# A streaming maximum over rows: one store moved to the end, the last row cut into two chained halves, all loads at one row pitch

## Chip, cores and metric

The kernel runs on one core of one Trainium2 chip. The metric is device time in microseconds (us); a profile of one execution goes with each kernel.

## The reference

```python
def setup_inputs():
    batch, seq, dim = 32, 512, 1024
    return {"x": np.random.randn(batch, seq, dim).astype(np.float32)}

def reference(x):
    return np.max(x, axis=-1).astype(np.float32)
```

This is 16384 rows of 1024 floats (4 KB each): 67.11 MB are read, 64 KB are written.

## The kernel before

Each of the 128 partitions takes 128 rows, in two blocks: 112 neighbouring rows (so neighbouring partitions lie 112 x 4 KB = 448 KB apart in `x`; this distance is called the pitch), then 16 rows (pitch 64 KB). A block is loaded in pieces of falling size through a ring of 46 rows per partition. VectorE reduces each piece. Each block has one store.

```python
BLOCKS = [
    [14, 14, 12, 11, 9, 8, 8, 7, 6, 5, 4, 4, 4, 3, 3],
    [2, 2, 2, 2, 2, 1, 1, 1, 1, 1, 1],
]
RING = 46
# ... (pools, shapes)
    at = first = 0
    for loads in BLOCKS:
        S = sum(loads)
        xb = xf[first * P:(first + S) * P, :].rearrange("(p i) d -> p i d", p=P)
        b = 0
        for g in loads:
            if at + g > RING:
                at = 0
            xc = ring[:, at:at + g, :]
            nc.sync.dma_start(out=xc, in_=xb[:, b:b + g, :])
            nc.vector.reduce_max(out=res[:, first + b:first + b + g], in_=xc, axis=X)
            at += g
            b += g
        dst = bass.AP(tensor=of.tensor, offset=of.offset + first * P, ap=[[S, P], [1, S]])
        nc.scalar.dma_start(out=dst, in_=res[:, first:first + S])
        first += S
```

## Time and profile before

| | before |
|---|---|
| time, median | 165.1 us (165.01 to 165.19, 6 runs) |
| span of the profiled run | 163.3 us |
| first load lands | 20.1 us after the start of the span |
| last store issued, landed | 160.91, 162.33 us |

In the profile lines of this document DVE is VectorE, SPq the queue that issues the loads, ACTq the one that issues the stores, and L50 a line of the kernel's source; `...` stands between lines of different views or for lines left out.

How to read the table: almost the whole span is one stream of loads that keeps all 16 DMA engines busy. Three stages can be told apart: how late the first load lands, how long the stream takes from its first landing to its last, and the tail after the last landing (last reduction, last store).

### The profile page before, as it was taken

What the parts mean: (1) busy time and instruction counts of PE and PEld (TensorE: products, weight loads), DVE (VectorE), ACT (ScalarE), POOL (GpSimd) and SP (SyncE); (2) the same over time, 40 slices, a digit from 0 to 9 for tenths busy, and PEclk for the clock granted to TensorE, in tenths of its full rate; (3) what the DMA queues carried; (4) which work ended last, traced back from release to release, by engine and by line L of the source; (5) the groups of instructions that cost most, each with busy time, mean ns of one, the idle gap of its engine ahead of it and who ended that gap; (6) DMA issues with size and microseconds to landing.
All of it is one profiled execution on the core that took longest, in us unless ns stands there. A gap on an engine that the chain in (4) does not pass through costs nothing.

```text
span 163.3 us, 109 instructions
## 1 busy us (share of the span) xinstructions
DVE 138.5 (85%) x26; POOL 0.2 (0%) x4
## 2 busy tenths in 40 slices
DVE  0000099969999999999999999999999999999994
POOL 0000000000000000000000000000000000000000
DMA  6999999998899897999989999999999999999980
GB/s 225 449 449 449 449 449 449 449 417 385 385 409 522 353 530 321 433 433 441 473 385 473 425 449 400 434 395 451 413 425 433 429 414 418 425 421 419 404 357 2
DMA packets 4032, 67.18 MB, mean 411 GB/s; under 512 B 704, under 2 KB 704, under 8 KB 1472
## 3 DMA queue, kind: packets, MB, share of 16 engines
q1 hardware_dynamic: 3744, 67.11, 96.4%
q10 hardware_dynamic: 288, 0.07, 0.2%
HBM read 67.11 MB, written 0.07 MB: 411 GB/s over the span
## 4 chain that ended last, share of the span: by engine, by line
DMA 57%; DVE 40%; DVEq 1%; SPq 0%; issue 0%
DMA ring<-in_x_dram 57%; DVE res L50 40%; DVEq L82 1%; SPq L49 0%
## 5 line engine op out<-in xcount | busy, mean ns | idle before, releaser
L50 DVE TENSOR_REDUCE res<-ring 128x1 f32<-128x1024 f32 (+11 forms) x26 | 138.5, 5396 | 22.4 <-DMA ring<-in_x_dram 22.4
L71 POOL MEMSET const-bfloat16-1.0<- 128x1 bf16 x1 | 0.1, 101 | 0.0
L71 POOL MEMSET const-uint8-127<- 128x1 uint8 x1 | 0.1, 101 | 0.0
L71 POOL MEMSET const-float32-0.0<- 128x1 f32 x1 | 0.1, 98 | 0.2 <-issue 0.2
L71 POOL MEMSET const-float32-1.0<- 128x1 f32 x1 | 0.1, 98 | 0.0
## 6 DMA issues: line engine op xcount, KB each, us to landing
ring<-in_x_dram SPq DMA_DIRECT2D x2, 7168.0 KB, 27.6
ring<-in_x_dram SPq DMA_DIRECT2D x2, 4096.0 KB, 31.6
ring<-in_x_dram SPq DMA_DIRECT2D x1, 6144.0 KB, 49.9
ring<-in_x_dram SPq DMA_DIRECT2D x3, 2048.0 KB, 36.8
ring<-in_x_dram SPq DMA_DIRECT2D x1, 5632.0 KB, 29.7
ring<-in_x_dram SPq DMA_DIRECT2D x5, 1024.0 KB, 24.6
ring<-in_x_dram SPq DMA_DIRECT2D x1, 4608.0 KB, 23.7
ring<-in_x_dram SPq DMA_DIRECT2D x1, 3584.0 KB, 38.4
```

Source lines behind the costliest of these rows:

```text
L50: nc.vector.reduce_max(out=res[:, first + b:first + b + g], in_=xc, axis=X)
L71: nc = _bacc.Bacc("TRN2", target_bir_lowering=False, num_devices=1)
L82: with _tile.TileContext(nc) as tc:
```

## The change

It has four parts. All loads get one pitch of 512 KB (128 rows per partition in one run). The last two-row and single-row loads are cut finer, so that eight single rows precede the last one. The last row of each partition is loaded as two halves into different buffers; the first half's maximum is written just ahead of the second half, so that the second reduction (513 elements) takes it in. And the first store now holds 127 of the 128 results per partition, so that it can't go out before the loads are nearly over; the last store then writes one float per partition. The intent is a stream without a store in it and less work after the last landing.

```diff
-BLOCKS = [
-    [14, 14, 12, 11, 9, 8, 8, 7, 6, 5, 4, 4, 4, 3, 3],
-    [2, 2, 2, 2, 2, 1, 1, 1, 1, 1, 1],
-]
-RING = 46
+ROWS = [14, 13, 11, 11, 9, 8, 8, 7, 6, 5, 5, 4, 4, 3, 3, 2, 2, 2, 2, 1, 1, 1, 1, 1, 1, 1, 1]
+RING = 45
+RUN = 128
 ...
+    xr = xf[:RUN * P, :].rearrange("(p i) d -> p i d", p=P)
+    out_r = bass.AP(tensor=of.tensor, offset=of.offset, ap=[[RUN, P], [1, RUN]])
+    if RUN == I:
+        x_last, out_last = xr[:, I - 1, :], out_r[:, I - 1:]
+    else:
+        x_last = xf[RUN * P:, :]
+        out_last = bass.AP(tensor=of.tensor, offset=of.offset + RUN * P, ap=[[1, P], [1, 1]])
 ...
+    PAD = 16
+    tail = once.tile([P, PAD + H], F32)
 ...   (loop over ROWS: load and reduce as before)
+    half = ring[:, at, :H]
+    nc.sync.dma_start(out=half, in_=x_last[:, :H])
+    nc.sync.dma_start(out=tail[:, PAD:], in_=x_last[:, H:])
+    nc.scalar.dma_start(out=out_r[:, :I - 1], in_=res[:, :I - 1])
+    nc.vector.reduce_max(out=tail[:, PAD - 1:PAD], in_=half, axis=X)
+    nc.vector.reduce_max(out=res[:, I - 1:], in_=tail[:, PAD - 1:], axis=X)
+    nc.scalar.dma_start(out=out_last, in_=res[:, I - 1:])
```

More of the change, by code (lines that the diff above doesn't have):

```diff
@@ L32 @@
     N, D = xf.shape
+    H = D // 2
     I = N // P
     of = out.flatten_outer_dims()
+    assert sum(ROWS) == I - 1 and RUN >= I - 1
+    xr = xf[:RUN * P, :].rearrange("(p i) d -> p i d", p=P)
[5 more added lines that the diff above has]
+        out_last = bass.AP(tensor=of.tensor, offset=of.offset + RUN * P, ap=[[1, P], [1, 1]])
     once = ctx.enter_context(tc.tile_pool(name="once", bufs=1))
@@ L38 @@
     res = once.tile([P, I], F32)
-    at = first = 0
-    for loads in BLOCKS:
-        S = sum(loads)
-        xb = xf[first * P:(first + S) * P, :].rearrange("(p i) d -> p i d", p=P)
-        b = 0
-        for g in loads:
-            if at + g > RING:
-                at = 0
-            xc = ring[:, at:at + g, :]
-            nc.sync.dma_start(out=xc, in_=xb[:, b:b + g, :])
-            nc.vector.reduce_max(out=res[:, first + b:first + b + g], in_=xc, axis=X)
-            at += g
-            b += g
-        dst = bass.AP(tensor=of.tensor, offset=of.offset + first * P, ap=[[S, P], [1, S]])
-        nc.scalar.dma_start(out=dst, in_=res[:, first:first + S])
-        first += S
-    assert first == I
+    PAD = 16
+    tail = once.tile([P, PAD + H], F32)
+    b = at = 0
+    for g in ROWS:
+        if at + g > RING:
+            at = 0
+        xc = ring[:, at:at + g, :]
+        nc.sync.dma_start(out=xc, in_=xr[:, b:b + g, :])
+        nc.vector.reduce_max(out=res[:, b:b + g], in_=xc, axis=X)
+        at += g
+        b += g
+    if at + 1 > RING:
+        at = 0
+    half = ring[:, at, :H]
[5 more added lines that the diff above has]
+    nc.scalar.dma_start(out=out_last, in_=res[:, I - 1:])
 _INS = ['x']
```

## The prediction

> **What bounds the kernel now.** I read the page first, then the chain in order of time, then windows over the loading stage, then the timeline and issues of the last microseconds. One core, no matmul: only VectorE (DVE), the load queue (issued from SP) and the store queue (issued from ACT) matter.
>
> The page of the kernel before, busy tenths and queues:
>
> ```profile
> span 163.3 us, 109 instructions
> DVE 138.5 (85%) x26; POOL 0.2 (0%) x4
> ...
> DMA  6999999998899897999989999999999999999980
> ...
> q1 hardware_dynamic: 3744, 67.11, 96.4%
> q10 hardware_dynamic: 288, 0.07, 0.2%
> ```
>
> The reader should see a DMA row without a hole from the first slice to the last but one, and the load queue q1 holding 96.4% of the time of all 16 engines. DVE works 138.5 of 163.3 us: it has slack overall. The chain of waits, in order of time, seems to say otherwise:
>
> ```profile
> 1.15 35.88 DMA ring<-in_x_dram
> ...
> 37.05 58.02 DVE res L50 x5
> ...
> 95.08 36.77 DMA ring<-in_x_dram
> ...
> 131.87 19.94 DMA ring<-in_x_dram
> ...
> 151.84 7.92 DVE res L50 x6
> 159.75 1.13 DVEq L82
> ```
>
> Its 58 us of DVE in the middle are not what sets the time: DVE lags behind the stream there, but the DMA engines never go idle, and at 95.08 the chain is back on the DMA. Only the end counts: from 151.84 on DVE reduces back to back until the last row. Windows (busy columns are DVE and POOL; the last three numbers are clock, share of the 16 DMA engines, GB/s):
>
> ```profile
> 40.00:95.00 55.00, 55.00 (x5) 0.00 (x0) 1.00 1.00 433
> 95.00:132.00 37.00, 36.78 (x8) 0.00 (x0) 1.00 0.99 425
> 132.00:139.00 7.00, 7.00 (x2) 0.00 (x0) 1.00 1.00 421
> 142.00:149.30 7.30, 7.30 (x4) 0.00 (x0) 1.00 1.02 422
> ...
> 152.00:158.00 6.00, 6.00 (x5) 0.00 (x0) 1.00 1.03 410
> ```
>
> The engines are always full; the rate sinks only because loads get smaller, from 433 GB/s for loads of 7 to 14 rows a partition to 410 for single rows. So the time is: about 158 us of saturated loading, then a tail of the last reduction and the last store. The tail, from the timeline and the issues of the last load pair and the last store:
>
> ```profile
> 151.84 9.04 DVE L50 TENSOR_REDUCE res<-ring 128x2 f32<-128x2048 f32 x7 [0.19 <-DMA ring<-in_x_dram]
> ...
> ring<-in_x_dram SPq DMA_DIRECT2D x2, 512.0 KB, 9.1
> ...
> 160.91 0.34 ACTq L54 DMA_DIRECT2D out_dram<-res x1
> ...
> out_dram<-res ACTq DMA_DIRECT2D x1, 8.0 KB, 1.4
> ```
>
> The last two loads were issued at 149.53 and 149.90 and took 9.1 us each in the median (8.7 for the first alone, so 9.5 for the second): the last lands at T = 159.4 to 159.5. The last reduction runs from 159.67 to 160.88, the store is issued at 160.91 and lands 1.4 us later, at 162.3; closing work fills the rest to 163.3.
>
> **What the Trainium skill says.** First, "DMA: Bandwidth & Descriptors", section "Where 436 GB/s comes from": 16 ports give 435.2 GB/s. The trace agrees, 433 GB/s with large loads, so the stream can't get much faster: 67.11 MB at 435.2 would take 154.2 us. Second, same page, section "Latency and other measured facts": copies from HBM to HBM at a row pitch of 512 KiB ran at 207 GB/s per direction, against 214 for a padded pitch (and 164 at 2 MiB); it calls the mechanism an inference. No run here shows a pitch of 512 KB; the trace shows pitches of 448 KB (112 rows of 4 KB, the first block) and 64 KB (the second block), both at full engine share. Third, same page, section "Anatomy of one DMA — SWDGE (gpsimd) path": a fixed cost of about 2 us, most of it the receipt of the write. The store here, from another queue, took 1.4 us. Fourth, "VectorE: DVE Perf Modes", section "The perf-mode tier table": a tensor reduction has only the 1x mode. The trace agrees:
>
> ```profile
> L50 DVE TENSOR_REDUCE res<-ring 128x14 f32<-128x14336 f32 x2 | 30.2, 15086 | 22.0 <-DMA ring<-in_x_dram 22.0
> ...
> L50 DVE TENSOR_REDUCE res<-ring 128x1 f32<-128x1024 f32 x6 | 6.8, 1208 | 0.0
> ```
>
> (15086 - 1208) / 13 rows = 1067.5 ns per 1024 elements, so 1.0425 ns each and 140 ns of fixed cost. Back to back the starts of single rows lie closer: the seven reductions from 151.84 take 9.04 us, and with 2.29 us for the first alone by the same timeline and some overlap, a single row costs 1.125 us on a busy DVE.
>
> **The change, part by part.**
>
> (a) More loads. 26 become 29 (27 of whole rows, two of half rows). Cost of one load: the two-row loads that released DVE at 149.36 and 151.84 lie 2.48 us apart; a single row at 410 GB/s takes 0.524 MB / 410 = 1.279 us. From a + 2b = 2.48 and a + b = 1.279: b = 1.20 us per row, a = 0.08 us per load. Three more loads: +0.23 us on the stream.
>
> (b) The first store leaves the stream. Before, it was issued at 142.87 and its packets ran among the loads:
>
> ```profile
> q10 hardware_dynamic: 144, 0.06, 4.2%
> ```
>
> That is the window from 145 to 150: 4.2% of 5.0 us = 0.21 us of all engines, taken from the loads. Now it waits for the 127th row's reduction, when the last load is about landing. -0.21 us. With (a): T moves by +0.02 us, to about 159.5.
>
> (c) Ring of 45 for 46, slightly smaller first loads. The fourth load now waits, as before, for the first reduction (ends 35.2), with 38 rows asked for. At 1.20 us a row those last until about 48. The sixth load waits for the third reduction, which I put at about 62, while the fifth has data until about 72. No hole; 0 us.
>
> (d) The DVE tail. Before, six single rows followed the last two-row load. The first started 0.94 us behind its landing (2.20 us of reduction against 1.28 us of loading) and each made up 1.28 - 1.125 = 0.155 us, so that the last started about 0.2 us behind. Now eight single rows precede the halves; the lag at the eighth is 0 to 0.2 us, say 0.1, because the two-row loads ahead, only four now, may not have emptied the backlog. Half rows land 0.08 + 0.60 = 0.68 us apart, so row 127 lands at T - 1.36 and its reduction starts at T - 1.26. The first half starts 1.125 later, T - 0.13, and takes 140 + 512 x 1.0425 = 674 ns: until T + 0.54. The second half reads the first's result, so it can't overlap; allow 0.03 us, as between the last reduction and the store's issue (160.88 to 160.91). It runs from T + 0.57 to T + 1.25, the store is issued at T + 1.28. Before it was T + 1.43 to 1.45. Gain 0.15 us, not the half row (0.5 us) that the idea promises, because DVE, not the landing, sets the last starts.
>
> (e) The last store writes 4 bytes per partition at a step of 512 bytes instead of 64 bytes. Packets are few either way; landing 1.4 us, perhaps 0.1 more. The first store (508 bytes per partition) is issued near T - 0.1, 1.4 us before the second, on the same queue: its issue of 0.34 to 0.38 us is over by then, and its packets, with idle engines, too. 0 to +0.1 us.
>
> Sum: +0.02 - 0.15 + 0.05 = -0.1 us: 165.0 us.
>
> **Rivals.**
>
> 1. The 512 KB pitch slows the stream. If the skill's ratio carried over, 157.5 us of loading would become 157.5 x 214 / 207 = 162.8, and the time 170.3, slower by 3.2%. For it: every partition's run starts at the same offset of a power of two, and so do the 16 engines' streams. Against: that figure has writes beside reads, the engines here sit at their own ceiling, and the 64 KB pitch of the last 16 rows, also a power of two, shows no loss (422 GB/s for two-row loads, on the trend from 421 for the three-row loads of the 448 KB block). I give any loss above 0.5 us 20%, above 3.3 us 7%.
>
> 2. The first store becomes the new wait: it now lies in the end, so its landing, or the two stores touching neighbouring words of the same output, might delay the second. Packets of the first would be done before those of the second start, by (e); at worst the second lands a store's 1.4 us later, 166.5 us.
>
> 3. DVE keeps up better than I think, the second half starts at its landing: store issue at T + 0.71, a gain of 0.7 us, 164.4 us. Against it: the backlog of 0.94 us after a two-row reduction is plain in the trace.
>
> **Range and chances.** The time is 165.0 us; no part of it is worth more than 0.3 us but the pitch. Below lies rival 3, half realised, 164.6; above, a mild loss by the pitch of 1% of the stream, 166.6. Faster by over 2% needs 161.8 us, less than the load stream and the unchanged tail leave room for: 0.01. Slower by over 2% needs 168.4, only the pitch can do that: 0.07. Within 2%: 0.92.
>
> **What would show it.** The window from 40 to 95 should still give 430 to 435 GB/s at full share (below 425: rival 1). The last load should land at 159.3 to 159.7. The two half reductions should read 670 to 680 ns, with no overlap; DVE should be back to back into the first half. The last store's issue should stand near 160.8, with the first store's 1.4 us earlier, and land within 1.5 us. A DMA hole in the middle would refute (c). I am wrong if the pitch costs, or if the last store lands late.

## The result

The changed kernel takes 165.36 us in the median (165.34 to 166.46, 6 runs), the kernel before 165.10 (165.01 to 165.19, 6 runs). The ratio is 1.0028, with a 95% interval of 1.0004 to 1.0053: 0.3% slower, far within 2%. (Ratios are computed as the mean time of one kernel's fast runs over that of the other's of the same rounds, so they are not quite the ratio of the medians. The one run of 166.46 is in it.) Predicted were 165.0 and a range of 164.6 to 166.6. The range holds; the sign of the small difference was wrong.

The windows of the changed kernel (columns: stretch, its length, busy time of VectorE and of POOL, clock, share of the 16 DMA engines, GB/s):

```profile
40.00:95.00 55.00, 53.94 (x6) 0.00 (x0) 1.00 1.00 433
95.00:132.00 37.00, 37.00 (x7) 0.00 (x0) 1.00 1.00 426
132.00:139.00 7.00, 7.00 (x3) 0.00 (x0) 1.00 0.99 418
142.00:149.30 7.30, 7.30 (x5) 0.00 (x0) 1.00 1.01 415
149.50:157.50 8.00, 8.00 (x7) 0.00 (x0) 1.00 1.03 409
```

The large loads run at 433 GB/s, as before. The stream as such is not slower at the new pitch. Now the beginning: the first load's issue to landing and the first reduction, which waits for it, in the kernel before:

```profile
ring<-in_x_dram SPq DMA_DIRECT2D x1, 7168.0 KB, 19.4
...
20.11 15.09 DVE L50 TENSOR_REDUCE res<-ring 128x14 f32<-128x14336 f32 x1 [20.11 <-DMA ring<-in_x_dram]
```

and in the changed kernel:

```profile
ring<-in_x_dram SPq DMA_DIRECT2D x1, 7168.0 KB, 19.9
...
20.63 15.09 DVE L56 TENSOR_REDUCE res<-ring 128x14 f32<-128x14336 f32 x1 [20.63 <-DMA ring<-in_x_dram]
```

The same 14 rows per partition land 0.52 us later. From this landing to the last one the stream takes 139.37 us before (20.09 to 159.46) and 139.36 after (20.61 to 159.97), as the last loads' issue plus time to landing also tell. So the whole surplus of the stream is there before its first landing. The tail of the changed kernel, from the timeline (start, duration, engine, operation) and the last stores' issue to landing:

```profile
158.71 1.22 DVE L56 TENSOR_REDUCE res<-ring 128x1 f32<-128x1024 f32 x1
159.85 0.68 DVE L66 TENSOR_REDUCE tail<-ring 128x1 f32<-128x512 f32 x1
159.97 0.38 ACTq L65 DMA_DIRECT2D out_dram<-res  x1
160.56 0.69 DVE L67 TENSOR_REDUCE res<-tail 128x1 f32<-128x513 f32 x1
161.28 0.34 ACTq L68 DMA_DIRECT2D out_dram<-res  x1
...
out_dram<-res ACTq DMA_DIRECT2D x1, 63.5 KB, 1.6
out_dram<-res ACTq DMA_DIRECT2D x1, 0.5 KB, 1.4
```

The reader should see that the first half starts before the single row ahead of it has quite ended (159.85 against 158.71 + 1.22), so VectorE is what it waits for, and that the second half starts only when the first is over. The store was issued 1.45 us after the last landing before (160.91 - 159.46), 1.31 after (161.28 - 159.97): the tail gained 0.14 us. The last store takes 1.4 us to land in both. Sum: +0.52 + 0.00 - 0.14 = +0.38 us up to the last store's issue, and 161.28 - 160.91 = 0.37. The time grew by less, 0.26 us: from the last store's landing to the end of the span 0.88 us pass in the changed kernel and 0.99 before (162.69 to 163.57, 162.33 to 163.32). What shortens this closing work was not looked into.

The chain of waits of the changed kernel ends so:

```profile
93.36 66.58 DVE res L56 x21
159.93 0.60 DVE tail L66
160.54 0.02 issue
160.56 0.69 DVE res L67
```

It gives VectorE 66 us in one piece, more than before, although the DMA engines are full in all these windows. As in the prediction, this is a chain that followed the wrong one of two things that keep pace with each other: the windows are full, and VectorE starts the eighth single row only 0.02 us behind its landing (158.71, landed 158.69), so up to there it has no backlog.

### The profile page after: what moved, and what is told of

Its sections match the earlier page's. It is cut to its first block, busy times and chain, and to the rows that moved or that the text cites. A ratio compares the mean times of both kernels' runs of the same rounds, so it can differ in the third digit from the quotient of the medians.

```text
span 163.6 us, 117 instructions
## 1 busy us (share of the span) xinstructions
DVE 138.9 (85%) x29; POOL 0.2 (0%) x4
## 4 chain that ended last, share of the span: by engine, by line
DVE 57%; DMA 40%; SPq 0%; issue 0%
DVE res L56 56%; DMA ring<-in_x_dram 40%; SPq L55 0%; DVE res L67 0%; DVE tail L66 0%
## 5 line engine op out<-in xcount | busy, mean ns | idle before, releaser
L67 DVE TENSOR_REDUCE res<-tail 128x1 f32<-128x513 f32 x1 | 0.7, 689 | 0.0
L66 DVE TENSOR_REDUCE tail<-ring 128x1 f32<-128x512 f32 x1 | 0.7, 676 | 0.0
```

Of the source, the lines that this page charges most:

```text
L66: nc.vector.reduce_max(out=tail[:, PAD - 1:PAD], in_=half, axis=X)
L67: nc.vector.reduce_max(out=res[:, I - 1:], in_=tail[:, PAD - 1:], axis=X)
```

## The experiments

Twelve runs were made; all gave correct results. One measure serves for all of them: the time from the start of the first reduction (the first load has landed) to the issue of the last store. It leaves out the beginning, the last store's landing and the closing work after it (from 0.81 us in b10 to 1.01 in six of the runs).

| kernel | pitch of the first load | first reduction | last store issued | difference | last store, issue to landing | time, median |
|---|---|---|---|---|---|---|
| before | 448 KB | 20.11 | 160.91 | 140.80 | 1.4 | 165.10 |
| changed | 512 KB | 20.63 | 161.28 | 140.65 | 1.4 | 165.36 |
| a1 (changed again) | 512 KB | 20.70 | 161.35 | 140.65 | 1.4 | 165.46 |
| a2 | 508 KB | 20.24 | 160.90 | 140.66 | 7.2 | 170.74 |
| a3 | 512 KB | 20.67 | 161.22 | 140.55 | 1.4 | 165.42 |
| a4 | 512 KB | 20.64 | 161.25 | 140.61 | 1.6 | 165.62 |
| b5 | 448 KB | 20.10 | 160.70 | 140.60 | 1.4 | 164.94 |
| b6 | 448 KB | 20.11 | 160.65 | 140.54 | 1.4 | 164.97 |
| b7 | 256 KB | 20.21 | 160.96 | 140.75 | 1.5 | 165.42 |
| b8 | 480 KB | 20.25 | 160.92 | 140.67 | 1.4 | 165.15 (one run) |
| b9 | 504 KB | 20.56 | 161.09 | 140.53 | 3.0 | 166.87 (one run) |
| b10 | 448 KB | 20.11 | 160.82 | 140.71 | 1.4 | 164.91 |
| c1 | 508 KB | 20.67 | 161.18 | 140.51 | 7.3 | 171.28 (one run) |
| c4 | 496 KB | 20.48 | 160.99 | 140.51 | 2.2 | 166.01 (one run) |

The theory after the first comparison: the delay of 0.5 us at the first landing comes from the 512 KB pitch. The rival: it is chance, or comes from something else in the changed kernel.

**a1: the changed kernel once more.** No edit.

> The changed kernel, unaltered, once more. In its profile all of the surplus of 0.5 us on the loading stood already at the landing of the first load (20.61 us after the start of the span against 20.09 before; the rest of the stream, from the first landing to the last, took 139.4 us in both). Theory A (the 512 KB pitch slows the first descriptors of the 16 engines): the first load lands at 20.5 to 20.7 again, the time is 165.3 to 165.5, 0.2 to 0.4 us over before. Theory B (the start is chance of one profile): the first landing moves by some tenths at random, and the miss must lie elsewhere.

Measured: first reduction at 20.70, time 165.46 us (165.31 to 165.51), ratio to before 1.0019 (1.0006 to 1.0031). The delay is no chance of one profile, and the rest of the kernel repeats too: 140.65 us both times.

**a2: runs of 127 rows, pitch 508 KB.**

```diff
-RUN = 128
+RUN = 127
```

> The changed kernel with runs of 127 rows per partition instead of 128: pitch 508 KB, the last row of each partition from the block of 128 contiguous rows at the end, the last store 512 contiguous bytes. Same sizes and number of loads, same reductions. Theory A (pitch): first load lands near 20.1, everything else as in the changed kernel, so 0.4 to 0.5 us faster than it, 164.9 us. Theory B (not the pitch): first landing as in the changed kernel, 165.3 to 165.4 us. The last store's place should not matter under either (landing 1.4 us).

Measured: 170.74 us (170.48 to 171.14, 4 runs), a ratio of 1.0342 (1.0328 to 1.0357) to before: slower by 5.6 us, which neither theory expected. The first reduction did start at 20.24, as theory A said, and the difference up to the last store's issue, 140.66, is that of the changed kernel. Everything is lost in the last store:

```profile
160.90 0.34 ACTq L68 DMA_DIRECT2D out_dram<-res  x1
...
out_dram<-res ACTq DMA_DIRECT2D x1, 63.5 KB, 2.0
out_dram<-res ACTq DMA_DIRECT2D x1, 0.5 KB, 7.2
```

The same 128 writes of 4 bytes that land after 1.4 us when they lie 512 bytes apart take 7.2 us when they lie side by side in 512 bytes. The time doesn't pass in the packets: this store lands at 168.09, and the six microseconds before 168 show no packet worth a hundredth of the DMA engines' time (the last two numbers, share and GB/s):

```profile
162.00:168.00 6.00, 0.00 (x0) 0.00 (x0) 1.00 0.00 0
```

My sentence that the last store's place should not matter was wrong; c1, b9, c4 and b8 follow it up.

**a3: the last row whole.**

```diff
-    half = ring[:, at, :H]
-    nc.sync.dma_start(out=half, in_=x_last[:, :H])
-    nc.sync.dma_start(out=tail[:, PAD:], in_=x_last[:, H:])
+    last = ring[:, at, :]
+    nc.sync.dma_start(out=last, in_=x_last)
     nc.scalar.dma_start(out=out_r[:, :I - 1], in_=res[:, :I - 1])
-    nc.vector.reduce_max(out=tail[:, PAD - 1:PAD], in_=half, axis=X)
-    nc.vector.reduce_max(out=res[:, I - 1:], in_=tail[:, PAD - 1:], axis=X)
+    nc.vector.reduce_max(out=res[:, I - 1:], in_=last, axis=X)
```

> The changed kernel with the last row loaded and reduced whole instead of in two chained halves. Theory C (the halves cost time, because the eighth single row already found DVE level with its landing): one load fewer takes 0.08 us off the stream, the last reduction starts 0.02 us after the landing and takes 1.21, so DVE ends 0.13 us earlier than with halves: 165.2 us, 0.1 to 0.2 faster than the changed kernel. Theory D (the halves gain, as they intend): 0.3 to 0.5 us slower than the changed kernel.

Measured: 165.42 us (165.27 to 165.59) against 165.46 of a1 on the same chip, not resolved. The trace resolves it: 140.55 against 140.65 us, so the whole row is 0.10 us faster than the halves. Most of that is the load saved: from first to last landing 139.30 us against 139.39 in a1 (139.36 in the first trace), and from the last landing to the store's issue 1.27 against 1.29 (1.31). Theory D (halves gain 0.3 to 0.5) is out; C is right in sign and nearly in size, but VectorE's own part, of which it expected 0.05, came to 0.01 to 0.04. The timeline of a3:

```profile
158.74 1.22 DVE L53 TENSOR_REDUCE res<-ring 128x1 f32<-128x1024 f32 x1
159.97 1.22 DVE L62 TENSOR_REDUCE res<-ring 128x1 f32<-128x1024 f32 x1
```

After eight single rows VectorE is level with the stream: the last reduction no longer overlaps the one ahead of it (158.74 + 1.22 is 159.96), it starts on its landing. With halves the first half landed while VectorE was still at the single row ahead (at 159.36, half a microsecond before its reduction started), and the chain of two took 161.28 - 159.85 = 1.43 us up to the store's issue, where the whole row took 161.22 - 159.97 = 1.25: the head start was used up.

**a4: the kernel before with its two blocks joined.**

```diff
 BLOCKS = [
-    [14, 14, 12, 11, 9, 8, 8, 7, 6, 5, 4, 4, 4, 3, 3],
-    [2, 2, 2, 2, 2, 1, 1, 1, 1, 1, 1],
+    [14, 14, 12, 11, 9, 8, 8, 7, 6, 5, 4, 4, 4, 3, 3, 2, 2, 2, 2, 2, 1, 1, 1, 1, 1, 1],
 ]
```

> The kernel before with its two blocks joined into one: the same 26 loads and reductions, pitch 512 KB for all, and one store at the end of 512 bytes per partition. It loses the store in the stream, -0.2 us. Theory A (pitch costs 0.5 us at the first load): first load lands near 20.6 and the time is 165.4, 0.3 us over before. Theory B: first load near 20.1 and 164.9 us, 0.2 under before.

Measured: first reduction at 20.64, as theory A has it, time 165.62 us, ratio 1.0037 (1.0023 to 1.0051). This is the kernel before, same loads in the same order, with nothing of the changed kernel but the pitch (and the store that the pitch brings):

```profile
20.64 15.09 DVE L49 TENSOR_REDUCE res<-ring 128x14 f32<-128x14336 f32 x1 [20.64 <-DMA ring<-in_x_dram]
```

So the later first landing comes with the layout and not with the rest of the change. The difference, 140.61 against 140.80, shows the store gone from the stream: -0.19. The time is 0.2 us over what I had expected: the store of 512 bytes per partition takes 1.6 instead of 1.4 us to land.

**b5: the kernel before, its first store late.** The loads have the same sizes and pitches, but one single row of the first block comes second to last, so that the store of that block waits for it.

```diff
-BLOCKS = [ ...two lists... ]
+SIZES = [112, 16]
+LOADS = [(0, g) for g in (14, 14, 12, 11, 9, 8, 8, 7, 6, 5, 4, 4, 4, 3)] + [(1, 3), (0, 2),
+    (1, 2), (1, 2), (1, 2), (1, 2), (1, 1), (1, 1), (1, 1), (1, 1), (0, 1), (1, 1)]
 ...   (load and reduce (block, rows) in this order; a block's store follows its last row)
```

> The kernel before with the same multiset of 26 load sizes, pitches of 448 and 64 KB and both stores, but one single row of the first block loaded second to last, so that the first store (448 bytes per partition) has to wait for its reduction and no longer runs among the loads. Theory E (the store in the stream costs the 0.21 us that the share of its packets says): the last load lands 0.2 us earlier than before, 159.25, first load at 20.1, time 164.9. Theory F (the store used holes and costs nothing): last landing 159.45, 165.1 us. If the first store now delays the second (rival 2 of the prediction), the last store takes over 1.6 us to land.

Measured: 140.60 against 140.80, so -0.20 us; the last load lands at 159.25 (159.46 before). Theory E, and the 0.21 us that the prediction had read from the packets' share, hold. The second store lands 1.4 us after its issue, undisturbed. Time 164.94 us (164.85 to 165.05), ratio 0.9989 (0.9976 to 1.0001): by the times alone it can't be told from the kernel before.

**b6: as b5, eight single rows.**

```diff
-    (1, 2), (1, 2), (1, 2), (1, 2), (1, 1), (1, 1), (1, 1), (1, 1), (0, 1), (1, 1)]
+    (1, 2), (1, 2), (1, 2)] + [(1, 1)] * 6 + [(0, 1), (1, 1)]
```

> As the kernel with the late store, with one two-row load split into two single rows, so that eight single rows end the stream as in the changed kernel: the candidate for the best version, without the 512 KB pitch and without halves. By the sums so far: one more load +0.08 on the stream, the last reduction starts 0.02 instead of 0.21 us behind its landing: 0.1 us under the late-store kernel, 164.8 us, 0.3 under before. If the singles don't help, 165.0.

Measured: 140.54, 0.06 us under b5; 164.97 us (164.76 to 165.17), ratio 0.9990 (0.9978 to 1.0003). One more load moved the last landing from 159.25 to 159.38, of which 0.02 stands at the first landing: 0.11 us for a load where I had 0.08. The last reduction starts 0.03 instead of 0.21 us behind its landing. It nets out to almost nothing.

**b7: two blocks of 64 rows, pitch 256 KB.**

```diff
 BLOCKS = [
-    [14, 14, 12, 11, 9, 8, 8, 7, 6, 5, 4, 4, 4, 3, 3],
-    [2, 2, 2, 2, 2, 1, 1, 1, 1, 1, 1],
+    [14, 14, 12, 11, 9, 4],
+    [4, 8, 7, 6, 5, 4, 4, 4, 3, 3, 2, 2, 2, 2, 2, 1, 1, 1, 1, 1, 1],
 ]
```

> The kernel before in two blocks of 64 rows per partition, so both at a pitch of 256 KB; two-block form kept, 27 loads, the first store (256 bytes per partition) in the stream, the second of 256 bytes at the end. If any large power of two delays the first descriptors: first load lands at 20.5 to 20.7, and there may be a second delay where the second block begins; 165.6 us. If 512 KB alone does: first load at 20.1, 165.2 us.

Measured: first reduction at 20.21, close to the 448 KB kernels. So it isn't every large power of two. Nor does its second block bring a delay: 140.75 with the store in the stream and one more load. Its time of 165.42 us (165.22 to 165.65), ratio 1.0019 (1.0005 to 1.0033), is 0.2 us more than its trace explains against before. The profiled execution itself took 165.23 us, though, and its span of 163.45 against 163.32 explains that one; the rest is how far the five executions differ.

**b9, c1, c4, b8: other splits into two blocks.** These have other pitches, and last stores of 8, 4, 16 and 32 bytes per partition without gaps. The edits move single rows from the second block to the first; b9 for one:

```diff
 BLOCKS = [
-    [14, 14, 12, 11, 9, 8, 8, 7, 6, 5, 4, 4, 4, 3, 3],
-    [2, 2, 2, 2, 2, 1, 1, 1, 1, 1, 1],
+    [14, 14, 12, 11, 9, 8, 8, 7, 6, 5, 4, 4, 4, 3, 3, 2, 2, 2, 2, 1, 1, 1, 1, 1, 1],
+    [1, 1],
 ]
```

> The kernel before in blocks of 126 and 2 rows per partition (pitch 504 KB, then 8 KB), 27 loads. The last store writes 8 bytes per partition into 1 KB without gaps. In the run with a pitch of 508 KB the last store, 4 bytes per partition into 512 bytes without gaps, landed 6.9 us after its issue had ended, where the same 4 bytes at steps of 512 bytes took 1.1. Theory G (writes of several partitions into the same 64 bytes go one after another, 16 writers there, 8 here): landing about half of the surplus, 2.5 to 3.5 us over 1.1. Theory H (the number of small writes close together counts, not the sharing): 5 to 6 us over 1.1 again. Theory I (only that store in that run, by its overlap with the first store): 1.1. First load near 20.1 us if the pitch alone matters for it.

> The kernel before in blocks of 127 and 1 rows per partition: pitch 508 KB once more, no halves, last store 4 bytes per partition into 512 bytes without gaps. If the slow last store was no chance, it lands 6 to 7 us after its issue again and the time is 170 to 171 us. First landing: 20.2 again if a pitch of 508 KB is free of the delay; 20.5 to 20.6 if the first landing at pitches around 500 KB is a matter of the run.

> The kernel before in blocks of 124 and 4 rows per partition: pitch 496 KB, last store 16 bytes per partition, so 4 writers to each 64 bytes (16 writers cost 5.8 us over the usual 1.1 from the end of the issue to the landing, 8 writers 1.5). If sharing of 64 bytes is what costs: 0.3 to 0.8 over 1.1. If only stores of under 16 bytes cost: 1.1. First landing: no theory is left that foretells it, between 20.1 and 20.6.

> Blocks of 120 and 8 rows per partition: pitch 480 KB, last store 32 bytes per partition, 2 writers to each 64 bytes: 0 to 0.3 us over 1.1. First landing 20.1 to 20.6, as above.

Measured, issue to landing of the last store of c1:

```profile
out_dram<-res ACTq DMA_DIRECT2D x1, 0.5 KB, 7.3
```

of b9:

```profile
out_dram<-res ACTq DMA_DIRECT2D x1, 1.0 KB, 3.0
```

of c4:

```profile
out_dram<-res ACTq DMA_DIRECT2D x1, 2.0 KB, 2.2
```

and of b8:

```profile
out_dram<-res ACTq DMA_DIRECT2D x1, 4.0 KB, 1.4
```

(The expectations count from the end of the issue, 0.34 us later than these figures.) The slow store repeats in c1, so it was no chance. Nor is it the overlap with the first store, the other half of theory I: in b9 and c4 the first store had landed (160.61, 159.96) before the last was issued (161.09, 160.99), and b5 and b6 have the overlap and take 1.4 us. All have 128 writes close together and differ by a factor of five in time, so their number alone doesn't decide, and H falls. The landing shrinks as fewer partitions write into the same 64 bytes: 16 writers 7.2 to 7.3 us, 8 writers 3.0, 4 writers 2.2, 2 writers and 1 writer (the kernel before) 1.4. That fits theory G in kind. Its size was not as foretold: b9 lies 1.6 us over 1.4, not 2.5 to 3.5. The size of the unit (64 bytes or another), the size of each write and how close all of them lie are not separated here, since they changed together; only the changed kernel (with a1 and a3) has 4-byte writes far apart, and they cost nothing extra.

The first landings of these runs break the neat form of theory A. The two runs at a pitch of 508 KB are the kernels a2 and c1:

```profile
20.24 15.09 DVE L56 TENSOR_REDUCE res<-ring 128x14 f32<-128x14336 f32 x1 [20.24 <-DMA ring<-in_x_dram]
```

```profile
20.67 15.09 DVE L50 TENSOR_REDUCE res<-ring 128x14 f32<-128x14336 f32 x1 [20.67 <-DMA ring<-in_x_dram]
```

At 504 KB it is 20.56, at 496 KB 20.48, at 480 KB 20.25. What holds is this: four of four traces at 448 KB lie between 20.10 and 20.11, four of four at 512 KB between 20.63 and 20.70. I can't say that these two pitches were traced on one chip; but on one chip, with the same sizes of the first loads (b10, b8, c4, c1), the first reduction starts later with each pitch, 448, 480, 496 and 508 KB: 20.11, 20.25, 20.48, 20.67, one trace each. (a2, early at 508 KB, ran on another chip and its second load has 13 rows instead of 14; which of these matters isn't shown.) The times can be compared on one chip as well. By its trace a4 should take 0.53 (first landing) - 0.19 (store) + 0.2 (last landing) = 0.5 us more than before, and on the same chip it took 165.62 against 165.13; without the delay it would have been level. What does not hold is that the power of two is the reason: 256 KB is early and 504 KB is late. I also looked for a cause in the first packets, of which each engine has at most one by then: up to 2.45 us, 16 had begun before and 12 in the changed kernel, but 14 in b5, whose first load landed early, and 16 in c1, whose landed late. So this doesn't sort them.

What does sort them is when these first packets end. Each of the 16 engines moves the first load in packets of 14 rows (57344 bytes). Nearly all first packets take 2.2 to 3.7 us, the later ones about 2.1, and an engine begins its second packet when its first ends. Here are the beginnings of the second packets, in slices of 0.05 us from 4.20 on (a digit other than 0 is a slice in which a packet began), in the kernel before and in the changed one:

```profile
DMA  0000009990999990000000000000000000000000
...
DMA  0000099099009990009009900900000000000000
```

Before, the last engine begins at 4.95, in the changed kernel at 5.45, while the earliest is no later (4.55 and 4.48). In all 14 traces the first load lands 15.1 to 15.2 us after the last of these beginnings. So the delay is not one of all engines: some of them lag, nearly all of the lag arises in their first packet, and a load has landed only when the last engine is through. The distance between the first and the last engine to finish a load is 0.4 us at the first load of the four kernels at 448 KB and 0.9 to 1.0 at 512 KB, and most of it is still there at the last load. Why the first packets take longer in some layouts stays open.

**b10: six half rows.** As b6, but the last three rows come as halves, all first halves ahead of all second halves, so that no reduction has to wait for the one just before it.

```diff
-... + [(1, 1)] * 6 + [(0, 1), (1, 1)]
+... + [(1, 1)] * 5
+    rows = [(1, 14), (0, 111), (1, 15)]
+    for n, (k, i) in enumerate(rows):      # first halves
+        nc.sync.dma_start(out=ring[:, at + n, :H], in_=xb[k][:, i, :H])
+        nc.vector.reduce_max(out=tails[n][:, PAD - 1:PAD], in_=ring[:, at + n, :H], axis=X)
+    for n, (k, i) in enumerate(rows):      # second halves
+        nc.sync.dma_start(out=tails[n][:, PAD:], in_=xb[k][:, i, H:])
+        nc.vector.reduce_max(out=res[:, c:c + 1], in_=tails[n][:, PAD - 1:], axis=X)
```

> The late-store kernel with eight singles (pitches of 448 and 64 KB), where the last three rows come as six half rows, all first halves before the second ones, so that each chained pair has two other reductions between. In the changed kernel the halves gained nothing because the first started 0.49 us behind its landing (1.14 us of DVE for the single row before it, 0.66 us between landings) and the second waited for the first. If that is the cause, six halves at 0.60 us each against 0.68 between landings bring the lag from 0.5 to about 0.05, DVE ends 0.75 us after the last landing instead of 1.24; three more loads cost 0.25. So 0.2 to 0.3 us under the kernel with eight singles, 164.7 us. If halves cost more than that on DVE, no gain: 165.0 or more.

Measured: 140.71, that is 0.17 us worse than b6, not 0.2 to 0.3 better; time 164.91 us (164.75 to 165.00), ratio 0.9989 (0.9975 to 1.0002). Its timeline:

```profile
154.89 2.33 DVE L47 TENSOR_REDUCE res<-ring 128x1 f32<-128x1024 f32 x2
157.14 1.86 DVE L57 TENSOR_REDUCE tail<-ring 128x1 f32<-128x512 f32 x3
158.92 1.87 DVE L61 TENSOR_REDUCE res<-tail 128x1 f32<-128x513 f32 x3
```

The step per half was right: three halves take 157.14 to 158.92, 0.59 us each, so chained halves do overlap when two others stand between. My error was the starting lag. I had taken the 0.5 us of the changed kernel, which has eight single rows ahead of its halves; here there are only five, and the trace has the first half 0.91 us behind its landing. Five further halves brought it down to 0.61 only. Against b6 the three added loads moved the last landing from 159.38 to 159.50, and VectorE ended 1.29 us after it instead of 1.24. Halves make up backlog more slowly per piece than whole rows do ((0.91 - 0.61) / 5 = 0.06 us against 0.15), so with a backlog they are no remedy, and without one a single row already starts on its landing.

**The best version.** b5, b6 and b10 all lie at 164.9 to 165.0 us, against 165.1 for before in the same rounds. All three point the same way, but each interval reaches 1. (b10 keeps level in time although its trace is 0.17 us behind b6 at the last store's issue: its closing work takes 0.81 us against 1.01.) They beat the changed kernel by their traces and by 0.4 us in the medians, though not in the same rounds. b5 is the simplest.

## Why the prediction was right or wrong

- **What bounds the kernel:** right. The stream sets the time; 139.37 and 139.36 us from first to last landing.
- **(a) more loads, (b) the store out of the stream:** right, +0.02 us foretold, -0.01 found. Apart: b5 gives -0.20 for the store (foretold -0.21), b6 gives 0.11 for one load (foretold 0.08). Three loads at 0.11 would make the sum +0.13, so the parts add up only to about 0.1 us, and that the sum hit this closely is partly luck.
- **(c) no hole in the middle:** right, the windows are full. But the paragraph, and the sum with it, silently took the first load's landing as unchanged, and this is the step that failed. A term is missing from the sum: +0.52 us ahead of the first landing. The sum with it is 165.1 + 0.02 - 0.15 + 0.05 + 0.52 = 165.5; measured were 165.36 and, in a1, 165.46. The sum lacks a second, smaller term, the closing work after the last landing, shorter by 0.1 us.
- **(d) the tail:** right. Foretold were a first half from T - 0.13 and a second from T + 0.57 to T + 1.25; the trace has, with T = 159.97, T - 0.12, T + 0.59 and T + 1.28. Two small errors cancel in this: the eighth single row lagged by 0.02 us instead of 0.1, and it landed at T - 1.28 instead of T - 1.36. The gain was 0.14 us. That the finer single rows alone give it, and the halves cost 0.10 us, most of it for one more load, I had not seen; a3 shows it.
- **(e) the last store:** right for this change, 1.4 us to landing. But only because its 4 bytes stay 512 bytes apart: side by side they took 5.8 us more in a2. The prediction had not asked this, so here it was lucky.
- **Rival 1 (the pitch):** wrong in the form in which I put it, as a loss of rate all along the stream. 433 GB/s in the window from 40 to 95 is the same at both pitches. The cost that came with the pitch is a single delay at the beginning, made in the first packets of some engines; why they take longer is open. It came to 0.52 us, just over the 0.5 us to which the prediction gave 20%.
- **Rival 2:** the first store did not disturb the second. **Rival 3:** the second half did not start at its landing, but 0.59 us later.
- **What would show it:** the full rate from 40 to 95, the step from one half to the other without overlap, VectorE back to back into the first half and the store's 1.4 us came as described. The second half took 689 ns, a little over the 670 to 680; the last landing (159.97 instead of 159.3 to 159.7) and the last store's issue (161.28 instead of 160.8) were late by the missing term.

## What to carry to other kernels

In a kernel that streams at the DMA engines' limit, split the span at the first and the last landing before comparing two versions: here a gain of 0.14 us in the tail, and one of 0.2 us from a store taken out of the stream that three more loads used up, were hidden by a loss of 0.52 us ahead of the first landing. Before cutting the last piece of work finer, look whether the last reduction starts on its landing or on the end of the one before. More single rows removed the backlog (0.21 to 0.03 us in b6); halves never paid here, since the first half found VectorE still at the row ahead (0.49 us in the changed kernel, 0.91 in b10) and each piece costs a load. And look where small stores land: several partitions writing into the same few dozen bytes can cost more than all the tuning of the tail.

## What the Trainium skill lacked or had wrong

- "DMA: Bandwidth & Descriptors", "Latency and other measured facts", row pitch: it gives 207 GB/s at 512 KiB against 214 at a padded pitch, 3% less, for copies from HBM to HBM. For loads from HBM on one core these runs show no such loss in the steady part (40 to 95 us: 431 to 434 GB/s at 448 KB, 431 to 433 at 512 KB). They show a later first landing of a load of 14 rows per partition (first reduction at 20.63 to 20.70 us against 20.10 to 20.11), and the page has nothing on that. The page's row is about large powers of two; this delay does not follow them (256 KB: 20.21, 504 KB: 20.56).
- The same page, "Specifications", says that below 512 bytes per transfer the engine does a read-modify-write, but no page says what it costs when several partitions write into the same small stretch of HBM: 128 writes of 4 bytes landed 7.2 to 7.3 us after their issue side by side, and after 1.4 us at steps of 512 bytes; 8, 16 and 32 bytes each, side by side, took 3.0, 2.2 and 1.4 us.
- The same page has a fixed cost per DMA for one alone, but no figure for one more load in a queue that is always full: 0.08 us by the kernel before, 0.11 by b6 against b5, 0.04 each for the three of b10 (159.50 - 159.38).
